# Where split weights lie in SBUF: wider tiles, two starting floats, and two norms side by side

## The chip, the cores and the metric

One core of a Trainium2 chip runs the whole program in one launch. The metric is the device time of one execution in microseconds (us); lower is better.

## The reference, cut to what matters

Two transformer blocks follow each other on 256 tokens of width 1024, all in float32.

```python
def first_block(...):
    ...
    yx, _, _ = mixer_sublayer(hx, kc, vc, rope, ...)
    x = x + g1 * yx
    h2 = modulate(rms_norm(x, norm2_g[l]), sh2, sc2)
    x = x + g2 * expert_choice_moe(h2, w_router[l], w_gate[l], w_up[l], w_down[l])
    return rms_norm(x, final_g)

def second_block(x, p, positions, norm_gains, ...):
    h = x
    for i in range(DEPTH_2):
        g = norm_gains[i]
        f = swiglu(rmsnorm(h, g[0]), ffn_gate[i, 0], ffn_up[i, 0], ffn_down[i, 0])
        h = h + MACARON * rmsnorm(f, g[1])
        mix = hybrid_mixer(rmsnorm(h, g[2]), ...)
        h = h + rmsnorm(mix, g[3])
        f = swiglu(rmsnorm(h, g[4]), ffn_gate[i, 1], ffn_up[i, 1], ffn_down[i, 1])
        h = h + MACARON * rmsnorm(f, g[5])
        gate = jax.nn.sigmoid(rmsnorm(h, g[6]) @ w_ple_gate[i])
        h = h + rmsnorm((p[i].astype(h.dtype) @ w_ple[i]) * gate, g[7])
    return h
```

So the first block's last norm (gain `final_g`) and the second block's first (gain `g[0]`) stand directly behind each other.

## The kernel before

The 256 tokens are two halves `h` of 128. Three stages follow each other: the first block's mixer, its sixteen experts, and the second block, which has two layers of feed-forward, mixer, feed-forward and a gated embedding (`ple`).

Large matrix products are made from split operands. `wsplit` (line 1168) takes a loaded weight tile `wt`, lets ScalarE (ACT) round it to a high part `wh` (line 1180) and VectorE (DVE) subtract that from the tile to give the low part `wl` (line 1181). Activations are split in the same way (`hh`, `hl` and others). `mm3` makes one product from three matmuls:

```python
        mm(out, lw[0], rw[0], start=start, stop=False, skip_group_check=skip)
        mm(out, lw[0], rw[1], start=False, stop=False, skip_group_check=skip)
        mm(out, lw[1], rw[0], start=False, stop=stop, skip_group_check=skip)
```

Its lines are 187, 188 and 189, for all products. The first operand is the stationary one (128 columns of weights for the array), the second moves through it (256 or 512 columns). There are three ways in which split weights are used:
- feature-major: `wh` is stationary, the activations move, 256 columns. This is the middle of each feed-forward (line 1329): column blocks 2 to 10, two halves, gate and up, eight steps `k` each; 864 matmuls in one go per feed-forward. The first mixer's hyena, Fourier and gate columns are made so too.
- token-major by columns (`by_k` and `tok_major`): the activations are stationary, `wh` moves, 256 columns. The first two column blocks of each feed-forward and the mixers' input projections.
- by rows (`rows_linear`): the activations are stationary, `wh` moves, 512 columns. Down, output and gate projections.

The tile pools set where a tile starts. `wh` and `wl` tiles have 1024 floats per partition, so all buffers of one pool start at the same float modulo 256; `shift` puts a small tile ahead of a pool.

At the border between the stages, `moe` adds the experts' sum `acc` to `x1`, half by half, and makes the two norms one behind the other: `norm_rstd` (square with a sum, root, reciprocal), the product with the first gain, then `pre_norm_half` (square, root, reciprocal, product with the gain at line 1212, scaling at 1215, transposes at 1218, split into `hh` and `hl` at 1221 and 1222). Meanwhile the first feed-forward's first four weight blocks (eight tiles) are split, and there `by_k` is given GpSimd (POOL) as the engine for the low parts (line 1309).

The order on each engine comes from the tile framework's scheduler and is fixed when the program is built. SyncE (SP) issues the weight loads in that order into rings of buffers; POOL issues the small loads (gains, embeddings) by the software queue, whose descriptors lie in a scratch area at the start of SBUF.

Of the kernel before, what the change touches and what calls it, by code (L numbers as in the profile page):

```python
# [11 lines left out]
F32 = mybir.dt.float32  # L12
F32R = mybir.dt.float32r
I32 = mybir.dt.int32
AF = mybir.ActivationFunctionType
OP = mybir.AluOpType
# [88 lines left out]
class Builder:  # L105
# [147 lines left out]
    def first_mixer(self, st):  # L253
# [5 lines left out]
        self.shift(WS, 24)  # L259
# [222 lines left out]
        def by_k(w):  # L482

            return [self.wsplit(w[:, 4 * i:4 * i + 4], (4, 256)) for i in range(2)]
# [476 lines left out]
    def moe(self, st):  # L961
# [87 lines left out]
        self.nwide = -1  # L1049
        for h in range(2):  # L1050
            for c in range(2):
                sl = slice(512 * c, 512 * c + 512)
                nc.vector.tensor_tensor(self.x1[:, h, sl], self.x1[:, h, sl], acc[h][c], op=OP.add)
            r = self.norm_rstd(self.h[:, h], self.wide(), D)
            nc.vector.scalar_tensor_tensor(self.h[:, h], self.h[:, h], r, self.fg, op0=OP.mult, op1=OP.mult)
            self.pre_norm_half(h, self.g0)
        self.dbg("h0", self.h)

    def second_tables(self, W):
# [13 lines left out]
        def rest():  # L1073
# [26 lines left out]
            nc.vector.tensor_copy(self.gcol, p[:, :16])  # L1100
            self.eps4 = C.tile([128, 1], F32, name="eps4")
# [3 lines left out]
            for i, t in enumerate((self.fg, self.g0)):  # L1105
                for c in range(2):
                    q = self.trps()
                    nc.tensor.matmul(q, self.ident[:2, i:i + 1].to_broadcast([2, 128]), rows[:, 512 * c:512 * c + 512], start=True, stop=True)
                    nc.vector.tensor_copy(t[:, 512 * c:512 * c + 512], q)

# [55 lines left out]
    def wsplit(self, src, shape, n=D, eng=None):  # L1166

        nc = self.nc
        self.nws += 1
        i = self.nws % sum(c for _, c in self.ws)  # L1170
        for pool, c in self.ws:
            if i < c:
                break
            i -= c
        hi = pool.tile([128, D], F32R, name="wh", tag="wh")[:, :n]
        lo = pool.tile([128, D], F32R, name="wl", tag="wl")[:, :n]
        if shape is not None:
            hi = hi.rearrange("p (a b) -> p a b", a=shape[0])
            lo = lo.rearrange("p (a b) -> p a b", a=shape[0])
        nc.scalar.activation(hi, src, AF.Copy)  # L1180
        (eng or nc.vector).tensor_tensor(lo, src, hi.bitcast(F32), op=OP.subtract)  # L1181
        return hi, lo

    def by_k(self, w, eng=None):

        return [self.wsplit(w[:, 4 * i:4 * i + 4], (4, 256), eng=eng) for i in range(2)]
# [20 lines left out]
    def pre_norm_half(self, h, g):  # L1207
# [4 lines left out]
        nc.vector.tensor_tensor(xn, self.h[:, h], g, op=OP.mult)  # L1212
        for q in range(2):
# [31 lines left out]
    def rows_linear(self, w, nk, lhs, step, tail=None):  # L1245
# [3 lines left out]
        def tile_k(k):  # L1249
            if k % 2 == 0:  # L1250
                ws["raw"] = self.load_rows(w, 128 * k)
            ws[k] = self.wsplit(ws["raw"][:, k % 2], None)
# [27 lines left out]
    def ffn(self, l, i):  # L1280
# [4 lines left out]
        with ExitStack() as FS:  # L1285
            self.shift(FS, 8)
# [19 lines left out]
            for h in range(2):  # L1306
                for c in range(2):
                    if h == 0:
                        pieces.append([self.by_k(self.load_cols(w, 256 * c), nc.gpsimd if l + i == 0 else None)
                                       for w in (wgt, wup)])  # L1310
# [10 lines left out]
            for c in range(2, NF // 2):  # L1321
                wg = self.load_cols(wgt, 256 * c)
                wu = self.load_cols(wup, 256 * c)
                for b in range(2):
                    p = self.gups()
                    for gi, w in ((0, wg), (1, wu)):
                        w2 = self.wsplit(w[:, :, 128 * b:128 * b + 128], (KD, 128))
                        for k in range(KD):
                            self.mm3(p[:, 256 * gi:256 * gi + 256], (w2[0][:, k], w2[1][:, k]), (hh[:, k], hl[:, k]),
                                     k == 0, k == KD - 1, skip=True)  # L1330
# [94 lines left out]
    def mixer(self, l):  # L1425
# [3 lines left out]
        with ExitStack() as XS:  # L1429
            self.shift(XS, 8)  # L1430
# [286 lines left out]
```

## Time and profile before

| | us |
|---|---|
| median of 3 runs | 2335.47 |
| lowest, highest | 2335.37, 2339.55 |
| the profiled execution | 2335.27 |
| its span | 2333.4 |

The profile is of one execution. PE is TensorE's matmuls, PEld its weight loads, which overlap with them. Matmuls are pipelined: one's record lasts longer than the distance to the next one's start. The tables by stretches give busy time, and in brackets the number of instructions that overlap with the stretch; PEclk is the granted clock of TensorE as a share of 2.4 GHz. A line number can be that of a helper.

### The profile page before, as it was taken

To read this page: it belongs to the slowest core of one execution; us is meant where nothing else is said; L and a number is where in the kernel's file an instruction comes from. 1 tells how busy PE (TensorE), PEld (TensorE's weight loads), DVE (VectorE), ACT (ScalarE), POOL (GpSimd) and SP (SyncE) were. 2 spreads that over 40 slices of the span, in tenths; PEclk is the share of its full clock that TensorE was granted. 3 is DMA by queue.
4 is the path that set the end of the run, shared out by engine and by line. 5 is a ranking of instruction groups with operands and counts; after the bars stand their busy time and mean duration, and the time that the engine had idled before them with its cause. 6 is when DMAs were issued, how large, how long until landed. Compare 5 with 4: busy or idle time off the path is not lost.

```text
span 2333.4 us, 31971 instructions
## 1 busy us (share of the span) xinstructions
PE 1913.6 (82%) x13520; PEld 1341.3 (57%) x13520; DVE 922.8 (40%) x1536; ACT 769.1 (33%) x1235; POOL 95.9 (4%) x111
## 2 busy tenths in 40 slices
PE   7899976666656666665656999999999999999998
PEld 4778932111111111111115998879987998879986
DVE  5855630100000000000005555676547654777555
ACT  5544420000000000000004444576437544676444
POOL 2100010000000000000004000100000000100000
PEclk9999988778676867677778999999999999999999
DMA  9466689999999999999997655436555554536551
GB/s 329 158 230 220 254 336 421 425 426 423 425 425 426 424 425 424 425 425 425 424 426 245 210 199 158 140 122 227 182 197 199 181 199 148 181 118 199 181 199 64
DMA packets 201203, 655.76 MB, mean 281 GB/s; under 512 B 10743, under 2 KB 141220, under 8 KB 164196
## 3 DMA queue, kind: packets, MB, share of 16 engines
q1 hardware_dynamic: 196772, 638.99, 71.4%
q0 software_dynamic: 4288, 14.72, 1.9%
q8 instruction: 106, 1.74, 0.3%
q14 instruction: 37, 0.30, 0.0%
HBM read 650.54 MB, written 3.15 MB: 280 GB/s over the span
## 4 chain that ended last, share of the span: by engine, by line
PE 49%; DMA 39%; DVE 6%; ACT 4%; issue 2%; SPq 0%; DVEq 0%; POOL 0%; ACTq 0%; POOLq 0%
DMA wt<-in_w_gate_dram 9%; DMA wp<-in_w_up_dram 9%; PE gu L187 7%; PE gu L188 7%; PE gu L189 7%; DMA wt<-in_w_up_dram 6%; DMA wp<-in_w_down_dram 5%; DMA wt<-in_w_down_dram 5%; DMA wp<-in_w_gate_dram 4%; PE acc L187 4%; PE acc L189 4%; PE acc L188 4%; DVE wl L1181 2%; PE mm L187 2%; PE mm L189 2%
## 5 line engine op out<-in xcount | busy, mean ns | idle before, releaser
L1181 DVE TENSOR_TENSOR wl<-wt,wh 128x1024 fp32r<-128x1024 f32 (+1 forms) x380 | 462.6, 1223 | 279.7 <-ACT wh L1180 277.6
L1180 ACT ACTIVATE wh<-wt 128x1024 fp32r<-128x1024 f32 x388 | 406.2, 1055 | 288.7 <-PE gu L188 112.9
L982 PE MATMUL gu<-wp,xg 128*32 128x512 f32 x1280 | 233.8, 869 | 156.3 <-DMA wp<-in_w_up_dram 99.5
L187 PE MATMUL gu<-hh,wh 128*128 128x256 f32 x1152 | 322.6, 280 | 0.0
L188 PE MATMUL gu<-hl,wh 128*128 128x256 f32 x1152 | 322.2, 280 | 0.0
L189 PE MATMUL gu<-hh,wl 128*128 128x256 f32 x1152 | 321.7, 279 | 0.0
L1007 ACT ACTIVATE a<-gu 128x512 f32<-128x512 f32 x16 | 9.6, 597 | 851.6 <-PE gu L982 851.6
L982 PEld LDWEIGHTS gu<-wp,xg 128*32 128x32 f32 x1280 | 43.4, 137 | 338.1 <-DMA wp<-in_w_up_dram 143.9
L1013 DVE TENSOR_TENSOR a<-a,gu 128x512 f32<-128x512 f32 x16 | 11.0, 688 | 564.4 <-PE gu L982 291.9
L187 PEld LDWEIGHTS gu<-hh,wh 128*128 128x128 f32 x1152 | 216.6, 188 | 0.0
L189 PEld LDWEIGHTS gu<-hh,wl 128*128 128x128 f32 x1152 | 216.2, 188 | 0.0
L188 PEld LDWEIGHTS gu<-hl,wh 128*128 128x128 f32 x1152 | 216.0, 187 | 0.0
L982 PE MATMUL gu<-wt,xg 128*32 128x512 f32 x768 | 129.8, 757 | 68.0 <-DMA wt<-in_w_up_dram 36.1
L1031 PE MATMUL tr<-wp,aT 128*32 128x256 f32 x1280 | 115.7, 525 | 55.4 <-DMA wp<-in_w_down_dram 52.2
L187 PE MATMUL acc<-wh,ah 128*128 128x512 f32 x352 | 139.1, 395 | 0.0
L189 PE MATMUL acc<-wh,al 128*128 128x512 f32 x352 | 138.1, 392 | 0.0
L188 PE MATMUL acc<-wl,ah 128*128 128x512 f32 x352 | 136.7, 388 | 0.0
L1037 DVE TENSOR_TENSOR y<-tr,g2b 32x256 f32<-32x256 f32 x64 | 26.9, 420 | 260.2 <-PE tr L1031 259.5
L1031 PEld LDWEIGHTS tr<-wp,aT 128*32 128x32 f32 x1280 | 50.1, 144 | 120.3 <-DMA wp<-in_w_down_dram 69.0
L982 PEld LDWEIGHTS gu<-wt,xg 128*32 128x32 f32 x768 | 20.3, 124 | 167.6 <-DMA wt<-in_w_gate_dram 76.2
L187 PE MATMUL acc<-wh,hh 128*128 128x256 f32 (+1 forms) x304 | 102.0, 336 | 1.1 <-ACT vd L1455 1.1
L189 PE MATMUL acc<-wh,hl 128*128 128x256 f32 (+1 forms) x304 | 99.2, 326 | 0.5 <-DVE hl L1222 0.5
(464 smaller groups left out, 3158.5 us busy)
## 6 DMA issues: line engine op xcount, KB each, us to landing
wp<-in_w_up_dram SPq DMA_DIRECT2D x48, 2048.0 KB, 27.5
wp<-in_w_down_dram SPq DMA_DIRECT2D x40, 2048.0 KB, 27.1
wt<-in_w_gate_dram SPq DMA_DIRECT2D x64, 1024.0 KB, 27.3
wp<-in_w_gate_dram SPq DMA_DIRECT2D x32, 2048.0 KB, 27.6
wt<-in_w_down_dram SPq DMA_DIRECT2D x48, 1024.0 KB, 27.6
wt<-in_ffn_gate_dram SPq DMA_DIRECT2D x44, 1024.0 KB, 6.5
wt<-in_ffn_up_dram SPq DMA_DIRECT2D x44, 1024.0 KB, 5.3
wt<-in_ffn_down_dram SPq DMA_DIRECT2D x44, 1024.0 KB, 4.9
```

The lines of the kernel that those rows point to most:

```text
L187: mm(out, lw[0], rw[0], start=start, stop=False, skip_group_check=skip)
L188: mm(out, lw[0], rw[1], start=False, stop=False, skip_group_check=skip)
L189: mm(out, lw[1], rw[0], start=False, stop=stop, skip_group_check=skip)
L982: mm((pga, pup)[g][32 * j:32 * j + 32, :], xg[2 * a + i][:, 32 * e:32 * e + 32], w[:, 512 * j:512 * j + 512], start=(done[g] == 1), stop=( ...
L1007: silu = nc.scalar.activation(a, pga, AF.Silu)
L1013: mul = nc.vector.tensor_tensor(a, a, pup, op=OP.mult)
L1031: mm(pd[32 * c:32 * c + 32, :256], aT[:, 2 * i + b, 32 * j:32 * j + 32], w[:, 1024 * b + 256 * c:1024 * b + 256 * c + 256], start=(t == 0) ...
L1037: nc.vector.tensor_tensor(y4[32 * r:32 * r + 32, 256 * c:256 * c + 256], pd[32 * c:32 * c + 32, :256], self.g2b[32 * c:32 * c + 32, 256 * ...
L1180: nc.scalar.activation(hi, src, AF.Copy)
L1181: (eng or nc.vector).tensor_tensor(lo, src, hi.bitcast(F32), op=OP.subtract)
```

## The change

Tiles of split weights are 64 floats wider (1088), so that successive buffers start 64 floats apart modulo 256, and `wsplit` places its 1024 floats at float 0 or 32 of the tile, by the argument `off`. The `shift` tiles change. The software queue's scratch is 4096 bytes per partition in place of 16384, which makes room. At the border, squares of the sum and of its product with the first gain are made side by side by halves of 512 columns; the second norm's root comes from both sums, its operand from the product of both gains (`fgg`, made in the expert stage), and the first norm's result `h` is written afterwards. The eight low parts that POOL made go to DVE. Scaling, transposes and split are now a function of their own, `to_operand`, with the same instructions.

```diff
@@ first_mixer
-        self.shift(WS, 24)
+        self.shift(WS, 56)
...
-            return [self.wsplit(w[:, 4 * i:4 * i + 4], (4, 256)) for i in range(2)]
+            return [self.wsplit(w[:, 4 * i:4 * i + 4], (4, 256), off=32) for i in range(2)]
@@ moe
         for h in range(2):
+            hv, xn = self.wide(), self.wide()
+            ms = W.tile([128, 2, 2], F32, name="ms", bufs=2)
             for c in range(2):
                 sl = slice(512 * c, 512 * c + 512)
-                nc.vector.tensor_tensor(self.x1[:, h, sl], self.x1[:, h, sl], acc[h][c], op=OP.add)
-            r = self.norm_rstd(self.h[:, h], self.wide(), D)
-            nc.vector.scalar_tensor_tensor(self.h[:, h], self.h[:, h], r, self.fg, op0=OP.mult, op1=OP.mult)
-            self.pre_norm_half(h, self.g0)
+                x2 = self.x1[:, h, sl]
+                nc.vector.tensor_tensor(x2, x2, acc[h][c], op=OP.add)
+                junk = W.tile([128, 512], F32, name="a")
+                nc.scalar.activation(junk, x2, AF.Square, scale=D ** -0.5, accum_out=ms[:, 0, c:c + 1])
+                nc.vector.tensor_tensor(hv[:, sl], x2, self.fg[:, sl], op=OP.mult)
+                nc.scalar.activation(hv[:, sl], hv[:, sl], AF.Square, scale=D ** -0.5, accum_out=ms[:, 1, c:c + 1])
+                nc.vector.tensor_tensor(xn[:, sl], x2, self.fgg[:, sl], op=OP.mult)
+            m = W.tile([128, 4], F32, name="mm", bufs=2)
+            nc.vector.tensor_tensor(m[:, 0:2], ms[:, :, 0], ms[:, :, 1], op=OP.add)
+            nc.vector.scalar_tensor_tensor(m[:, 2:3], m[:, 0:1], EPS, m[:, 1:2], op0=OP.mult, op1=OP.add)
+            nc.scalar.activation(m[:, 2:3], m[:, 2:3], AF.Sqrt, bias=self.eps2, scale=1.0)
+            nc.vector.reciprocal(m[:, 2:3], m[:, 2:3])
+            self.to_operand(h, xn, m[:, 2:3])
+            nc.scalar.activation(m[:, 3:4], m[:, 0:1], AF.Sqrt, bias=self.eps, scale=1.0)
+            nc.vector.reciprocal(m[:, 3:4], m[:, 3:4])
+            nc.vector.scalar_tensor_tensor(self.h[:, h], self.h[:, h], m[:, 3:4], self.fg, op0=OP.mult, op1=OP.mult)
@@ second_tables
+            self.fgg = W.tile([128, D], F32, name="fgg", bufs=1)
+            nc.vector.tensor_tensor(self.fgg, self.fg, self.g0, op=OP.mult)
@@ wsplit
-        hi = pool.tile([128, D], F32R, name="wh", tag="wh")[:, :n]
-        lo = pool.tile([128, D], F32R, name="wl", tag="wl")[:, :n]
+        hi = pool.tile([128, D + 64], F32R, name="wh", tag="wh")[:, off:off + n]
+        lo = pool.tile([128, D + 64], F32R, name="wl", tag="wl")[:, off:off + n]
...
-        (eng or nc.vector).tensor_tensor(lo, src, hi.bitcast(F32), op=OP.subtract)
+        nc.vector.tensor_tensor(lo, src, hi.bitcast(F32), op=OP.subtract)
@@ pre_norm_half
         nc.vector.tensor_tensor(xn, self.h[:, h], g, op=OP.mult)
+        self.to_operand(h, xn, r)
+
+    def to_operand(self, h, xn, r):
...
@@ rows_linear
-            ws[k] = self.wsplit(ws["raw"][:, k % 2], None)
+            ws[k] = self.wsplit(ws["raw"][:, k % 2], None, off=32)
@@ ffn
-            self.shift(FS, 8)
+            self.shift(FS, 48)
...
-                        pieces.append([self.by_k(self.load_cols(w, 256 * c), nc.gpsimd if l + i == 0 else None)
-                                       for w in (wgt, wup)])
+                        pieces.append([self.by_k(self.load_cols(w, 256 * c)) for w in (wgt, wup)])
...
-                        w2 = self.wsplit(w[:, :, 128 * b:128 * b + 128], (KD, 128))
+                        w2 = self.wsplit(w[:, :, 128 * b:128 * b + 128], (KD, 128), off=32)
@@ mixer
-            self.shift(XS, 8)
+            self.shift(XS, 16)
@@ kernel
-    nc = _bacc.Bacc("TRN2", target_bir_lowering=False, num_devices=1)
+    nc = _bacc.Bacc("TRN2", target_bir_lowering=False, num_devices=1, dynamic_dma_scratch_size=4096)
```

Distances as the pools place the tiles: start of the moving operand less start of the stationary operand of the next matmul, in floats of a partition, modulo 128 (from one `k` to the next it moves by 128). In brackets, matmuls in the whole program that are followed by another of their kind.

| moving, then stationary | columns | before | now |
|---|---|---|---|
| `hh`, `hl` on `wh`, `wl`: feed-forward's middle (3448) | 256 | 16 | 48, 112 |
| `wh`, `wl` on `hh`, `hl`: token-major, second block (1444) | 256 | 112 | 48, 112 |
| `wh`, `wl` on `ah`, `al`: down projection (1048) | 512 | 80 | 0, 64 |
| `wh`, `wl` on `hh`, `hl`: output and gate projection (382) | 512 | 112 | 16, 80 |
| `xh`, `xl` on `wh`, `wl`: first mixer, early (327) | 256 | 16 | 48, 112 |
| the same, later (431) | 256 | 48 | 48, 112 |
| `wh`, `wl` on `xh`, `xl`: first mixer, q, k, v (139) | 256 | 112 | 48, 112 |
| `wh`, `wl` on `mT`: first output projection (91) | 512 | 0, 80 | 0, 16, 64, 80 |

The order of instructions differs at the border alone. DVE before, from the add of the experts' sum to the second half's scaling (`x_70` is `x1`, `nr` a reciprocal root, `nt` a work tile):

```order
L1053 TENSOR_TENSOR x_70<-x_70,acc 128x512 x4
L1204 RECIPROCAL nr<-nr 128x1
L1055 SCALAR_TENSOR_TENSOR x_70<-x_70,nr,gain 128x1024
L1212 TENSOR_TENSOR nt<-x_70,gain 128x1024
L1204 RECIPROCAL nr<-nr 128x1
L1215 TENSOR_SCALAR nt<-nt,nr 128x512 x2
L1222 TENSOR_TENSOR hl<-tr,hh 128x4x128
L1204 RECIPROCAL nr<-nr 128x1
L1055 SCALAR_TENSOR_TENSOR x_70<-x_70,nr,gain 128x1024
L1222 TENSOR_TENSOR hl<-tr,hh 128x4x128
L1212 TENSOR_TENSOR nt<-x_70,gain 128x1024
```

DVE now, the same place, from the second half's first sums to the second column block's first low parts:

```order
L1240 TENSOR_SCALAR nt<-nt,mm 128x512 x2
L1072 SCALAR_TENSOR_TENSOR x_70<-x_70,mm,gain 128x1024
L1065 TENSOR_TENSOR mm<-ms 128x2
L1201 TENSOR_TENSOR wl<-wt,wh 128x1024
L1247 TENSOR_TENSOR hl<-tr,hh 128x4x128 x2
L1063 TENSOR_TENSOR nt<-x_70,fgg 128x512 x2
L1066 SCALAR_TENSOR_TENSOR mm<-mm 128x1
L1071 RECIPROCAL mm<-mm 128x1
L1201 TENSOR_TENSOR wl<-wt,wh 128x1024
L1068 RECIPROCAL mm<-mm 128x1
L1072 SCALAR_TENSOR_TENSOR x_70<-x_70,mm,gain 128x1024
L1240 TENSOR_SCALAR nt<-nt,mm 128x512 x2
```

The products at 1063 and the low parts at 1201 have come in between; the product with the first gain (1055, now 1072) stands behind the scaling.

POOL before, at the same place:

```order
L1071 DMA grows<-in_norm_gains_dram 1x16x64
L1181 TENSOR_TENSOR wl<-wt,wh 128x1024 x7
L1115 DMA gain<-in_norm_gains_dram 128x1024
L1181 TENSOR_TENSOR wl<-wt,wh 128x1024
L1115 DMA gain<-in_norm_gains_dram 128x1024
```

POOL now:

```order
L1087 DMA grows<-in_norm_gains_dram 1x16x64
L1135 DMA gain<-in_norm_gains_dram 128x1024 x2
L1500 DMA lg<-in_q_norm_dram 128x256
L1501 DMA lg<-in_kv_norm_dram 128x128
L1586 MEMSET qz 128x2048
```

The eight low parts are gone from POOL, and the two gain loads stand first.

## Rows read from the trace of the kernel before

**Rows 1.** The page: busy time with its share, and PE's busy tenths by slice.

```profile
PE 1913.6 (82%) x13520; PEld 1341.3 (57%) x13520; DVE 922.8 (40%) x1536; ACT 769.1 (33%) x1235; POOL 95.9 (4%) x111
...
PE   7899976666656666665656999999999999999998
```

**Rows 2.** The chain that ended last, at the border: start us, us, what.

```profile
1242.01 1.30 DVE x L1053 x2
...
1251.10 4.88 DVE nt L1215 x2
...
1265.26 1.10 PE tr L1218 x8
```

**Rows 3.** PE by stretches: us, busy (x), PEclk, DMA share, GB/s; feed-forward's middles.

```profile
1290.00:1380.00 90.00, 90.00 (x766) 1.00 0.58 194
...
2142.00:2232.00 90.00, 90.00 (x767) 1.00 0.58 196
```

**Rows 4.** Instructions in order of time, in a middle: start us, us, engine, line.

```profile
1380.02 0.28 PE L187 MATMUL gu<-hh,wh 128*128 128x256 f32 x1
1380.02 0.19 PEld L188 LDWEIGHTS gu<-hl,wh 128*128 128x128 f32 x1
```

**Rows 5.** PE by stretches, other 256-column runs; distances: 112, 16, 48, 48, 112, 112.

```profile
48.00:60.80 12.80, 12.80 (x116) 1.00 1.09 355
91.00:104.00 13.00, 13.00 (x113) 1.00 0.73 259
193.00:208.00 15.00, 15.00 (x130) 1.00 0.92 276
215.00:267.00 52.00, 52.00 (x461) 1.00 0.61 196
...
1459.20:1467.00 7.80, 7.80 (x68) 1.00 0.60 202
...
2134.30:2139.20 4.90, 4.90 (x46) 1.00 0.94 298
```

**Rows 6.** PE in order of time, entry into the last feed-forward's middle.

```profile
2138.48 0.28 PE L187 MATMUL gu<-hh,wh 128*128 128x256 f32 x1
...
2139.16 0.28 PE L187 MATMUL gu<-hh,wh 128*128 128x256 f32 x1
...
2140.09 0.28 PE L188 MATMUL gu<-hl,wh 128*128 128x256 f32 x1
...
2140.80 0.28 PE L188 MATMUL gu<-hl,wh 128*128 128x256 f32 x1
```

**Rows 7.** PE with 512 columns, in order of time, then a down projection by stretches.

```profile
277.39 0.39 PE L187 MATMUL wo<-wh,mT 128*128 128x512 f32 x1
...
280.57 0.39 PE L189 MATMUL wo<-wh,mT 128*128 128x512 f32 x1
...
1558.95 0.39 PE L187 MATMUL acc<-wh,hh 128*128 128x512 f32 x1
...
1575.75 0.39 PE L187 MATMUL acc<-wh,hh 128*128 128x512 f32 x1
...
1388.00:1445.00 57.00, 57.00 (x250) 1.00 0.46 149
```

**Rows 8.** Groups by line at the border (1238 to 1268 us): busy us, mean ns.

```profile
L1181 POOL TENSOR_TENSOR wl<-wt,wh 128x1024 fp32r<-128x1024 f32 x8 | 22.4, 2821 | 895.5 <-ACT wh L1180 895.4
...
L1215 DVE TENSOR_SCALAR nt<-nt,nr 128x512 f32<-128x512 f32 x4 | 7.7, 1968 | 0.1
```

**Rows 9.** Groups by line and form, border and second block (from 1230 us).

```profile
L1181 DVE TENSOR_TENSOR wl<-wt,wh 128x1024 fp32r<-128x1024 f32 x322 | 393.3, 1226 | 240.1 <-ACT wh L1180 238.0
...
L1222 DVE TENSOR_TENSOR hl<-tr,hh 128x512 fp32r<-128x512 f32 x32 | 20.7, 685 | 7.0 <-ACT hh L1221 7.0
L1215 DVE TENSOR_SCALAR nt<-nt,nr 128x512 f32<-128x512 f32 x32 | 20.1, 670 | 0.2
...
L1204 DVE RECIPROCAL nr<-nr 128x1 f32<-128x1 f32 x33 | 5.2, 157 | 5.6 <-ACT nr L1203 4.0 <-ACT nr L1201 1.5
```

More of the change, by code (lines that the diff above doesn't have):

```diff
@@ L1100, in rest @@
             nc.vector.tensor_copy(self.gcol, p[:, :16])
+            self.eps2 = C.tile([128, 1], F32, name="eps2")
+            nc.vector.memset(self.eps2, EPS * EPS)
             self.eps4 = C.tile([128, 1], F32, name="eps4")
@@ L1164, in wide, with wsplit @@
         return pool.tile([128, D], F32, name="nt", tag=tag, bufs=3 if tag == "nt" else 1)
-    def wsplit(self, src, shape, n=D, eng=None):
+    def wsplit(self, src, shape, n=D, off=0):
         nc = self.nc
@@ L1180, in wsplit, with by_k @@
         nc.scalar.activation(hi, src, AF.Copy)
-        (eng or nc.vector).tensor_tensor(lo, src, hi.bitcast(F32), op=OP.subtract)
+        nc.vector.tensor_tensor(lo, src, hi.bitcast(F32), op=OP.subtract)
         return hi, lo
-    def by_k(self, w, eng=None):
-        return [self.wsplit(w[:, 4 * i:4 * i + 4], (4, 256), eng=eng) for i in range(2)]
+    def by_k(self, w):
+        return [self.wsplit(w[:, 4 * i:4 * i + 4], (4, 256)) for i in range(2)]
     def tok_major(self, out, h, pieces):
@@ L1212, in pre_norm_half @@
         nc.vector.tensor_tensor(xn, self.h[:, h], g, op=OP.mult)
+        self.to_operand(h, xn, r)
+    def to_operand(self, h, xn, r):
+        nc = self.nc
         for q in range(2):
```

## The prediction

> **What bounds the kernel now.** I read the page's busy shares and slices first. TensorE (PE) is busy in 82% of the span: at nine tenths in slices 3 to 5, the first mixer, at five or six from slice 7 to 22, and at nine from slice 23 on, the second block [rows 1]. In the middle the expert stage waits for weights, and no edit moves those. So the change is worth what it does to PE in the first mixer and in the second block, and at the border between the two, where PE idles.
>
> That border I read in the chain of waits [rows 2]. From 1242.01 us, when the experts' sum is complete, to 1265.26, when the second half's transposes start, the chain is on VectorE (DVE): adds, the two norms, scalings. The reader is to see 4.88 us for two scalings of 128x512.
>
> In the second block I asked how fast PE goes while it waits for nothing. The table by stretches counts the matmuls of each stretch; since a matmul lasts 0.28 us (0.39 with 512 columns) and one that began just before is counted too, the pitch from one start to the next is (stretch + duration) / count. In the feed-forward's middle, four stretches of 90 us: 90.28 / 766 or 767 = **117.8 ns** for 256 columns, at clock 1.00, PE never idle [rows 3]. 256 columns at 2.4 GHz are 106.7 ns. So some 11 ns per matmul are neither columns nor waiting.
>
> What else goes on in a matmul's time is the next one's weight load: both records start at the same moment [rows 4]. Both read SBUF, the moving operand along one row of floats and the weights along another, so the distance of these two, which the change sets, is a possible cause. I therefore read the pitch of the same instruction elsewhere against the distances in the table of the change. At 16 (modulo 128) 13.28 / 113 = 117.5. At 48 it is 52.28 / 461 = 113.4 over 52 us, but also 15.28 / 130 = 117.5 over 15 us. At 112 it is 13.08 / 116 = 112.8, 8.08 / 68 = 118.8, 5.18 / 46 = 112.6 [rows 5]. Of 17 such stretches at 48 or 112 ten lie near 113 and seven near 118; the row shows its first, its last and the clearest. So there are **two speeds**, and a stretch keeps the one it has. Entering the last feed-forward the pitch is 113 (six matmuls in 0.68 us) although the distance is already 16; after one pause for a transpose it is 118 (six in 0.71), and stays so [rows 6]. All four middles begin with such a pause and all four are slow. So at 16 a pause ends at 118 ns each time I can see, at 48 or 112 in less than half of them.
>
> With 512 columns there is no such memory, and the distance shows plainly. At 0: 14 matmuls from 277.39 to 280.57, 227.1 ns. At 112: 72 from 1558.95 to 1575.75, 233.3 ns. At 80, the down projection: 57.39 / 250 = 229.6, and 228.6 with the 251 that one of the four gives; I take 229 [rows 7].
>
> **The parts.** One profiled execution took 2335.27 us; the sum is made against that. It is 0.2 us under the median of the runs, which is 2335.47.
>
> 1. Feed-forward middles. 3448 matmuls go from 16 to 48 and 112. Bounds: nothing (the pitch stays at 117.8) and 3448 x (117.8 - 113.4) = 15.2 us. I take 15.2: the long stretch at 48 is the nearest row, it too goes through hundreds of matmuls. DVE and ScalarE have time for it; a tile of 24 matmuls would take 2.72 us, and its split 1.23 us on DVE [rows 9]; DMA moves 194 to 196 GB/s there [rows 3].
>
> The rule that speaks against this part: the Trainium skill, page "SBUF — State Buffer", section "SBUF: two separate sides", has contention on the engine side only at the port pair that VectorE and GpSimd share, and says that TensorE never waits on anyone; a later section gives it a second, independent read port for weight loads. By that, the distance would be worth nothing and parts 1 to 3 would be 0. The trace speaks against it where distance alone differs, 227.1, 229 and 233.3 ns [rows 7].
>
> 2. Rows. The down projections' 1048 matmuls go from 80 to 0 and 64: 1048 x (229 - 227.1) = 2.0 us. Output and gate projections, 382 at 112, go to 16 and 80: 382 x (233.3 - 229) = 1.6 us. No row has 16 or 64 with 512 columns; bounds are 227.1 and 233.3, so from 4.4 us gained to 4.5 lost on the first (half of them at 64) and the second together; I take each as its neighbour modulo 64, as 48 and 112 behave alike.
>
> 3. First mixer: 327 matmuls with xh and xl go from 16 to 48 and 112, at most 327 x 4.4 = 1.4 us. PE is the chain there; I take 1.
>
> 4. Token-major columns, 1444 matmuls, stay at 48 or 112: 0, with 1444 x 4.4 / 2 = 3 us either way, as runs fall on the one or the other pitch.
>
> 5. Border. GpSimd's eight lo splits, 2821 ns each, go to DVE at 1226 [rows 8, 9], 9.8 us more for DVE. While GpSimd ran them, DVE's four scalings took 1968 ns each [rows 8]; all 32 of the block have 20.1 us, so the other 28 have (20.1 - 7.7) / 28 = 0.44 [rows 9]. New DVE work up to the eighth split: four adds, eight products, four hi/lo differences of 128x512 at 0.685 (11.0 us), four scalings at 0.44 (1.8), two 128x1024 products at a split's 1.23 (2.5), nine small ones at a reciprocal's 0.157 (1.4), eight splits (9.8) and two 128x256 items of the first column block (0.7, at half a 128x512 each) [rows 9]: 27.2 us, so from 1242.0 to 1269.2. PE then lacks 12 matmuls of the second column block: 1270.6. Before, that block began at 1266.11, after eight transposes [rows 2], and took 48 x 0.1156 = 5.5 us, the mean of the two speeds: 1271.6. So **1 us** gained; the first matmuls come sooner, but behind them stands the queue of splits. Bounds: 4 us gained, if PE's order hides the late splits, and 3 lost, if each small step between ScalarE and DVE stalls DVE's queue, which is served in order. The norms' own order (the second root no longer behind the first) is inside this.
>
> 6. The product of the two gains (1.2 us, as a split) and a memset lie in the expert stage, where DVE idles. The smaller DMA scratch and the wider tiles give no engine work; if the software queue's ring became too short, GpSimd's issues would wait. The same DMAs are issued in the same order on SP. I take 0.
>
> Sum: 15.2 + 2.0 + 1.6 + 1.0 + 1.0 = 20.8 us; 2335.3 - 20.8 = **2314.5 us**.
>
> **Rivals.**
> B. The middles are fast in part: two of the four, or half of each, 7.6 us less gain: 2322. For it: one pause decides, and at 112 both outcomes occur [rows 5].
> C. The state, not the distance, rules 256 columns, and the pauses that open the middles leave them slow as before. Part 1 is 0: 2335.3 - 5.6 = 2329.7. If distance is worth nothing anywhere, only the border is left: 2334.3. (That is the time by the Trainium skill's rule of part 1, which the 512-column rows contradict.) For C: all four middles agree now, at the same place of the program, as if the kind of pause decided; and 16 gave 113 for some matmuls [rows 6]. Against: 16 with a pause is never seen fast.
> D. Slower. Before, each stream had one distance; now each tile of 1088 floats moves it by 64. If every such step is a new chance for 118 ns, streams that are fast now become slow: of the 1444 token-major matmuls the fast half, 3.2 us; the first mixer's 461 of the long stretch at 48 [rows 5], 2.0 us; the down projection's half at 64 as bad as 112, 524 x 4.3 = 2.3 us; the middles gain nothing and the border gives 1. Together 2335.3 + 6.5 = 2342. It decides when a stream cannot keep 113 ns over one tile, that is 24 matmuls. Against: in the fast stretches both distances modulo 256 follow each other all the time, and 512 columns change speed within three matmuls.
>
> **How the numbers follow.** Forecast 0.52, B 0.20, C 0.19, D 0.09. A measurement of this kernel tells some 0.2%, 4.7 us, from no change. The forecast's own range, with parts 2, 4 and 5 at their bounds, is 2308 to 2320. To hold 8 in 10 the range must take in B and the part of C that keeps parts 2 and 3: 2308 to 2332. Faster by over 0.2% (under 2330.8) are the forecast, B and half of C: 0.81; within 0.2% the rest of C and a sliver of D: 0.11; slower 0.08.
>
> **What would show it.** Right: the four middles at 90.28 / 113.4 = 796 matmuls in 90 us in place of 766; the down projection's 57 us stretch with 252 or 253; output projection at 229; no GpSimd split, DVE's scalings at 0.44 at the border, and the first middle's start 1 us sooner. Wrong: a count of 766 in the middles (C), a mixture among the four (B), token-major stretches all at 118 or down at 233 (D), or PE waiting at the border for a lo tile beyond 1271 us.

## The result and the profile after

| | before | after |
|---|---|---|
| median, us | 2335.98 | 2312.84 |
| the profiled execution | 2335.27 | 2310.14 |
| its span | 2333.4 | 2308.4 |

The ratio is 0.9894 with a 95% interval of 0.9875 to 0.9913: faster by 1.1%. One of the four executions after was slow (2828.68 us, granted clock 0.63); it is in the median of the table but not in the ratio, which goes by the other three, with a median of 2311.20 us. Forecast were 2314.5 us and 20.8 us of gain; the profiled executions differ by 25.1.

The page after, busy time and PE's busy tenths by slice:

```profile
PE 1875.6 (81%) x13520; PEld 1322.4 (57%) x13520; DVE 923.0 (40%) x1556; ACT 768.1 (33%) x1243; POOL 73.7 (3%) x103
...
PE   7899966656556655665556999899999999999998
```

PE does the same 13520 matmuls in 38 us less busy time (1913.6 in [rows 1]); DVE's busy time is the same although it has eight low parts more. Not all of the 38 us is gain: 14.0 of it are the experts' matmuls at L982 (363.6 us before, 349.6 after), in a stage that waits for weights. What is gain shows in the stretches after, the four middles and one down projection (us, then busy time with the number of instructions for PE, PEld, DVE, ACT and POOL, then PEclk, DMA share, GB/s):

```profile
1284.00:1374.00 90.00, 90.00 (x796) 90.00 (x795) 52.76 (x67) 44.56 (x66) 0.00 (x0) 1.00 0.60 202
1596.00:1686.00 90.00, 90.00 (x796) 90.00 (x796) 52.76 (x66) 44.53 (x66) 0.00 (x0) 1.00 0.61 202
1810.00:1900.00 90.00, 90.00 (x796) 90.00 (x796) 52.77 (x66) 44.61 (x66) 0.00 (x0) 1.00 0.62 205
2122.00:2212.00 90.00, 90.00 (x796) 90.00 (x796) 52.67 (x66) 44.51 (x67) 0.00 (x0) 1.00 0.62 206
...
1378.00:1435.00 57.00, 57.00 (x253) 47.21 (x252) 26.44 (x26) 24.36 (x30) 0.00 (x0) 1.00 0.45 145
```

766 or 767 matmuls in 90 us [rows 3] have become 796, the number forecast: 90.28 / 796 = 113.4 ns, at the same clock. The down projection has 253 in 57 us where [rows 7] has 250: 57.39 / 253 = 226.8 ns.

The border, PE in order of time, from the experts' last gather products (L1042) over the second norm's transposes to the first token-major matmul, and the first matmul of the first middle:

```profile
1238.89 3.74 PE L1042 MATMUL acc<-y,back 128*128 128x512 f32 x8 [0.97 <-DVE y L1037]
1248.23 1.94 PE L1243 MATMUL tr<-ident,nt 128*128 128x128 f32 x8 [5.59 <-DVE nt L1240]
1250.75 0.58 PE L187 MATMUL gu<-wh,hh 128*128 128x256 f32 x1 [0.58 <-ACT hh L1246]
...
1278.62 0.28 PE L187 MATMUL gu<-hh,wh 128*128 128x256 f32 x1
```

I call the distance from the first L1042 to the first middle "the border": 1278.62 - 1238.89 = 39.7 us. In the trace before it runs from 1239.95 to 1285.61, 45.7. The border is 5.9 us shorter, and 5.0 of that lie ahead of the first token-major matmul (11.86 us behind L1042, before 1256.80 - 1239.95 = 16.85). These are one execution each; a second one of the change has 40.9 us (below), so a difference of about a microsecond between borders tells nothing.

### The profile page after: what moved, and what is told of

The parts are those of the page before. It is cut to its first block, busy times and chain, and to the rows that moved or that the text cites. A ratio compares the mean times of both kernels' runs of the same rounds, so it can differ in the third digit from the quotient of the medians.

```text
span 2308.4 us, 31994 instructions
## 1 busy us (share of the span) xinstructions
PE 1875.6 (81%) x13520; PEld 1322.4 (57%) x13520; DVE 923.0 (40%) x1556; ACT 768.1 (33%) x1243; POOL 73.7 (3%) x103
## 4 chain that ended last, share of the span: by engine, by line
PE 49%; DMA 40%; DVE 6%; ACT 4%; issue 1%; SPq 0%; DVEq 0%; POOL 0%; ACTq 0%; POOLq 0%
DMA wt<-in_w_gate_dram 10%; DMA wp<-in_w_up_dram 7%; PE gu L187 7%; PE gu L189 7%; PE gu L188 7%; DMA wt<-in_w_down_dram 6%; DMA wp<-in_w_down_dram 6%; DMA wt<-in_w_up_dram 5%; PE acc L187 4%; PE acc L189 4%; PE acc L188 4%; DMA wp<-in_w_gate_dram 2%; DVE wl L1201 2%; PE mm L187 1%; PE mm L189 1%
## 5 line engine op out<-in xcount | busy, mean ns | idle before, releaser
L1201 DVE TENSOR_TENSOR wl<-wt,wh 128x1024 fp32r<-128x1024 f32 x388 | 472.1, 1223 | 264.8 <-ACT wh L1200 261.6
L982 PE MATMUL gu<-wp,xg 128*32 128x512 f32 x1280 | 227.2, 847 | 157.8 <-DMA wp<-in_w_up_dram 103.2
L982 PEld LDWEIGHTS gu<-wp,xg 128*32 128x32 f32 x1280 | 42.8, 135 | 335.7 <-DMA wp<-in_w_up_dram 144.4
L982 PE MATMUL gu<-wt,xg 128*32 128x512 f32 x768 | 122.4, 716 | 78.2 <-DMA wt<-in_w_up_dram 41.3
L982 PEld LDWEIGHTS gu<-wt,xg 128*32 128x32 f32 x768 | 19.5, 121 | 170.6 <-DMA wt<-in_w_gate_dram 79.3
L187 PE MATMUL gu<-wh,hh 128*128 128x256 f32 (+1 forms) x336 | 98.4, 294 | 1.1 <-ACT hh L1246 1.1
```

Of the source, the lines that this page charges most:

```text
L982: mm((pga, pup)[g][32 * j:32 * j + 32, :], xg[2 * a + i][:, 32 * e:32 * e + 32], w[:, 512 * j:512 * j + 512], start=(done[g] == 1), stop=( ...
L1201: nc.vector.tensor_tensor(lo, src, hi.bitcast(F32), op=OP.subtract)
```

## The experiments

Two questions were open. Is it the distance of the operands that sets the pitch, and not the pause ahead of a stretch (rival C) or the stepping of the buffers (rival D)? And what made the border gain 5.9 us where 1.0 was forecast?

### Maps of the distance

`e1_map_a` and `e2_map_b` make the tiles of the second block 1152 floats wide, a multiple of 128, so that no buffer steps, and choose the starting float by a table, for each feed-forward or mixer and each use:

```diff
-                        w2 = self.wsplit(w[:, :, 128 * b:128 * b + 128], (KD, 128), off=32)
+                        w2 = self.wsplit(w[:, :, 128 * b:128 * b + 128], (KD, 128), off=OFF['mid'][2 * l + i])
-        hi = pool.tile([128, D + 64], F32R, name="wh", tag="wh")[:, off:off + n]
+        hi = pool.tile([128, wd], F32R, name="wh", tag="wh")[:, off:off + n]
```

The low part's tile, token-major columns and rows are edited alike.

> The changed kernel, with split tiles of the second block 128 floats wider (so every buffer has the same start modulo 128) and the starting float chosen per use: the four feed-forward middles get the distances 0, 32, 64, 96, the four down projections 32, 96, 48, 16, the output and gate projections 0, 64, 32, 96. Theory A, the distance of the moving operand to the next stationary one sets the pitch: the four middles differ from each other although the same instructions run in the same places; a distance keeps one pitch through 800 matmuls, 113.4 or 117.8 ns or a third value; with 512 columns 227 to 233.4 ns, each projection at one value. Theory C, the pause that opens a middle decides and not the distance: all four middles agree, at 117.8 as before the change or at 113.4 as after it, and 512 columns too show nothing that goes with the distance. Theory D, it is the stepping of buffers by 64 floats that keeps the middles fast: without stepping all four are at 117.8.

> As the run before, with middles at 80, 48, 16, 112, down projections at 112, 64, 0, 80, output and gate projections at 48, 112, 16, 80. Theory A: the third middle (16) at 117.8 ns, the second (48) and the fourth (112) at 113.4, the first (80) not known; the down projections at 233.4, 227, 227.1 and 229 ns in this order. Theory C: all four middles alike, whichever. Theory D: all four at 117.8, since no buffer steps. A middle at 16 that runs at 113.4, or one at 48 at 117.8, refutes A.

The stretches of the first map, middles at 0, 32, 64, 96:

```profile
1290.00:1380.00 90.00, 90.00 (x752) 90.00 (x751) 49.91 (x63) 42.46 (x64) 0.00 (x0) 1.00 0.57 187
1608.00:1698.00 90.00, 90.00 (x761) 90.00 (x760) 50.70 (x63) 42.10 (x63) 0.00 (x0) 1.00 0.59 196
1830.00:1920.00 90.00, 90.00 (x752) 90.00 (x751) 50.07 (x63) 41.87 (x62) 0.00 (x0) 1.00 0.58 191
2152.00:2242.00 90.00, 90.00 (x761) 90.00 (x760) 50.27 (x64) 42.94 (x64) 0.00 (x0) 1.00 0.58 190
```

Of the second map, middles at 80, 48, 16, 112, then down projections at 112, 64, 0, 80:

```profile
1286.00:1376.00 90.00, 90.00 (x767) 90.00 (x766) 51.12 (x64) 42.90 (x64) 0.00 (x0) 1.00 0.58 193
1606.00:1696.00 90.00, 90.00 (x796) 90.00 (x796) 52.78 (x66) 44.54 (x66) 0.00 (x0) 1.00 0.61 205
1820.00:1910.00 90.00, 90.00 (x766) 90.00 (x765) 50.92 (x63) 42.68 (x64) 0.00 (x0) 1.00 0.59 196
2136.00:2226.00 90.00, 90.00 (x796) 90.00 (x795) 52.78 (x66) 44.27 (x65) 0.00 (x0) 1.00 0.62 204
...
1384.50:1441.50 57.00, 57.00 (x246) 45.94 (x245) 24.99 (x23) 22.95 (x28) 0.00 (x0) 1.00 0.45 144
1700.80:1757.80 57.00, 57.00 (x253) 47.21 (x252) 26.43 (x26) 24.36 (x30) 0.00 (x0) 1.00 0.45 149
1919.30:1976.30 57.00, 57.00 (x253) 47.20 (x252) 26.43 (x26) 24.34 (x30) 0.00 (x0) 1.00 0.45 144
2232.40:2289.40 57.00, 57.00 (x251) 46.77 (x250) 25.88 (x25) 23.88 (x29) 0.00 (x0) 1.00 0.39 131
```

The same instructions, in the same places of one program, at clock 1.00 with PE never idle: 752, 761, 767 or 796 in 90 us, by the distance alone. In ns, with a period of 64 floats, since 64 gives what 0 gives and so on:

| distance modulo 64 | 0 | 16 | 32 | 48 |
|---|---|---|---|---|
| 256 columns | 120.0 | 117.8 | 118.7 | 113.4 |
| 512 columns | 226.8 | 229 | 232.3 | 233.3 |

(512 columns at 32 and 48 from the first map's down projections: 247 and 246 in 57 us.) Each map was run once; the times were 2344.27 and 2325.94 us. For the middles and for 512 columns theory A stands, C and D fall: the second middle of `e2_map_b` is at 113.4 with buffers that don't step, its third at 117.8.

In the middles only the weights moved, since `hh` and `hl` start at the same float modulo 64 in all runs. So it could be the weights' own place that counts, and not the distance. The token-major columns of the two maps speak against that: there the weights are the moving operand, and start elsewhere for the same distance. At 0, in the mixer of the second block's first layer of `e2_map_b`, the stretch is

```profile
1459.00:1464.00 5.00, 5.00 (x44) 5.00 (x43) 1.92 (x2) 3.35 (x7) 0.00 (x0) 1.00 0.28 96
```

5.28 / 44 = 120.0 ns; at 16 most stretches of the maps are at 117.8, at 32 they are at 118.5 to 119.0, about as in the middles. The order is opposite for the two widths: 48 is best for 256 columns and worst for 512. So weights that serve both need two places, which is what the argument `off` gives.

`e5_map_c` and `e6_map_d` are the same kernel with other numbers in the table.

> The kernel of the first two maps with finer steps: the four middles at 40, 44, 52, 56, the down projections at 4, 8, 56, 60, token-major columns of the feed-forwards at the middles' distances, of the mixers at 36 and 60, output projections at 8 and 56, gate projections at 4 and 60. The two maps gave, at 0, 16, 32, 48 modulo 64, for 256 columns 120.0, 117.8, 118.7 and 113.4 ns, for 512 columns 227, 229, 232.3 and 233.3. If the pitch is a smooth function of the distance with a period of 64 floats, 40 and 44 lie between 118.7 and 113.4, 52 and 56 between 113.4 and 120.0, and 4, 8, 56, 60 with 512 columns between 227 and 229 or 227 and 233.3. If only the class of 16 floats counts (a block that operands share), 40, 44 equal 32 or 48, and 52, 56, 60 equal 48: steps, not slopes. A distance where 256 columns are faster than 113.4, or one without the second pitch of 117.8, would be worth moving to.

> As the run before, with middles at 60, 36, 24, 8, down projections at 40, 24, 12, 20, token-major columns of the feed-forwards at 60, 36, 46, 50, of the mixers at 54 and 42, output projections at 2 and 62, gate projections at 6 and 40. Smooth: 60 near 118 to 120, 36 near 118, 24 between 117.8 and 118.7, 8 between 117.8 and 120. Steps of 16: 60 at 113.4 like 48, 36 at 118.7 like 32, 24 at 117.8 like 16, 8 at 120.0 like 0.

Between the multiples of 16 nothing is smooth, and nothing better (2341.93 and 2341.75 us). Middles in 85 us, `e5_map_c` at 52, the worst that was seen:

```profile
1830.00:1915.00 85.00, 85.00 (x691) 85.00 (x690) 46.02 (x60) 39.20 (x58) 0.00 (x0) 1.00 0.55 179
```

and `e6_map_d` at 60 and at 8:

```profile
1290.00:1375.00 85.00, 85.00 (x720) 85.00 (x720) 47.95 (x60) 40.27 (x61) 0.00 (x0) 1.00 0.58 194
...
2153.00:2238.00 85.00, 85.00 (x731) 85.00 (x730) 48.95 (x62) 40.58 (x61) 0.00 (x0) 1.00 0.58 192
```

85.28 / 691 = 123.4, 85.28 / 720 = 118.4, 85.28 / 731 = 116.7 ns. The others lie at 118.4 to 119.9, and both forecasts missed: with a slope 52 would lie below 120.0 and 8 above 117.8, with steps of 16 the distances 52, 56 and 60 would give 113.4. With 512 columns a down projection at 60 runs at 226.8 like one at 0, but a gate projection at 60 (35 matmuls of `e5_map_c`, from 2309.44 to 2317.48 us) at 236.5, which the expectation of `e12_map_e` puts at 234.5. Both have the same distance and other starts. So off the multiples of 16 the distance does not tell the pitch.

`e12_map_e` asks the same on the multiples: the down projection's operands and weights both move by 8 floats, middles stay at 48.

```diff
-            self.shift(FS, 48)
+            self.shift(FS, 56)
```

> The kernel of the maps with the down projection's operands moved by 8 floats, and the weights with them: the four down projections have the distances 0, 16, 32, 48 as in the maps, but both operands start at multiples of 16 floats, where all starts so far were at 8 more. Middles all at 48, token-major columns at 48 and 112, output and gate projections at 0 and 64. If the distance alone counts: 227, 229, 232.3 and 233.3 ns. If the start itself counts (which would explain why distances between the multiples of 16 gave 226.8 at 60 in one place and 234.5 in another), at least one of the four is elsewhere by over 1 ns. For what decides between 113.4 and 117.8 at 48: if a fixed place of every buffer were enough, all token-major stretches agree; if the pause decides anew each time, they are mixed as in the change, and the middles are at 113.4 four times of four again.

Its down projections, at 0, 16, 32, 48:

```profile
1381.80:1438.80 57.00, 57.00 (x253) 47.23 (x252) 26.41 (x26) 24.35 (x30) 0.00 (x0) 1.00 0.45 146
1693.90:1750.90 57.00, 57.00 (x251) 46.77 (x250) 25.88 (x25) 23.88 (x29) 0.00 (x0) 1.00 0.44 150
1907.40:1964.40 57.00, 57.00 (x247) 46.23 (x246) 25.17 (x24) 23.15 (x28) 0.00 (x0) 1.00 0.45 145
2221.00:2278.00 57.00, 57.00 (x246) 45.94 (x245) 24.94 (x23) 22.96 (x28) 0.00 (x0) 1.00 0.38 131
```

253, 251, 247, 246: the same four values (2315.36 us in all, one run). With 512 columns and distances that are multiples of 16 the distance is enough in all down projections, wherever the pair lies. Among the output and gate projections of the maps one doesn't fit by 1 ns: the last gate projection of `e1_map_a`, at 96, has 233.4 where 32 and 96 have 232.3 to 232.4 elsewhere; why stays open.

### Two numbers alone

`e9_two_numbers` is the kernel before, tiles 1024 wide, with

```diff
-        self.shift(st, 16, "right")
+        self.shift(st, 48, "right")
...
-            self.shift(FS, 8)
+            self.shift(FS, 56)
```

> The kernel before with two numbers changed: the small tile ahead of the second block's split tiles has 48 floats in place of 16, the one ahead of the down projection's operands 56 in place of 8. Tiles stay 1024 floats wide, no starting float, scratch and border as before. Distances: middles 48, down projections 0, output and gate projections 80, token-major columns 80 (before 112). Theory A by the maps: middles 3448 x 4.4 = 15.2 us, down 1048 x 2.2 = 2.3, output and gate 382 x 4.2 = 1.6 gained, token-major 1444 at 116 to 117.8 in place of 115.2, 1 to 3.8 us lost: 2318 to 2321 against 2335.3, ratio 0.993 to 0.994. If wide tiles and the starting float are what the gain needs, nothing or little is gained.

Measured were 2321.94 us beside 2338.13 for the kernel before, ratio 0.9931 (0.9917 to 0.9946), which is within theory A's 0.993 to 0.994. Its first middle:

```profile
1292.00:1382.00 90.00, 90.00 (x796) 90.00 (x795) 52.55 (x65) 44.53 (x66) 0.00 (x0) 1.00 0.62 206
```

The middles gain all they can. The price is in the token-major matmuls, which now have 80: those that follow each other directly average 117.7 ns, 115.2 before the change, and 1444 x 2.5 is 3.6 us lost. By the ratios, wide tiles and the starting float are worth what lies between 0.9931 here and 0.9912 for the whole layout without the new border (next section), some 4 us: they buy these back, no more. Since the scratch is that of before, a smaller one isn't what the middles gain by.

### The border

`e3_border_only` puts the new border, with the small scratch, into the kernel before; two shift tiles keep its distances. `e4_layout_only` puts the border of before into the changed kernel, whose small scratch it keeps.

```diff
@@ e3_border_only, against before
+            (the changed kernel's lines in moe, eps2, fgg, to_operand)
-                        pieces.append([self.by_k(self.load_cols(w, 256 * c), nc.gpsimd if l + i == 0 else None)
+                        pieces.append([self.by_k(self.load_cols(w, 256 * c), None)
-            self.shift(FS, 8)
+            self.shift(FS, 128)
-            self.shift(XS, 8)
+            self.shift(XS, 128)
@@ e4_layout_only, against the change: the reverse, in moe and in by_k
```

> The kernel before with the border alone changed: norms side by side, the eight low parts on VectorE, the small scratch; tiles, starting floats and distances as before. By the prediction's sum the border is worth 1.0 us: 2334.3. By the trace of the change, in which the first middle's start gained 5.8 us more than the experts' end did, it is worth 5.8 us: 2329.5, ratio 0.9975. In both the four middles stay at 117.8 ns and the down projections at 229. If the border's gain came from the distances (first column blocks faster), it would be absent here: 2335.

> The changed kernel with the border of before put back: norms one behind the other, the eight low parts on GpSimd; distances as in the change. Theory A: middles at 113.4 ns, down projections at 227; 15.2 + 2.0 + 1.6 + 1.0 = 19.8 us gained, 2315.5, ratio 0.9915. If a part of the gain in the middles needs the other border (order of buffers, state handed on), the first middle is at 117.8 and the time 3.8 us more, 2319.3. If parts add up, this run's gain and that of the border alone sum to the change's 23 to 25 us.

The border alone: 2332.19 us, ratio 0.9977 (0.9968 to 0.9987), some 5.4 us gained, not 1.0. The layout alone: 2317.42 us, ratio 0.9912 (0.9897 to 0.9926), 20.6 us gained, where theory A said 19.8. Together 26.0, and the change gives 24.8 (0.0106 x 2336): the parts add up within the intervals.

`e7_pool_lo` and `e8_old_norm` are the change with one half of the border put back: the low parts on GpSimd, or the norms one behind the other.

```diff
@@ e7_pool_lo
-                        pieces.append([self.by_k(self.load_cols(w, 256 * c)) for w in (wgt, wup)])
+                        pieces.append([self.by_k(self.load_cols(w, 256 * c), nc.gpsimd if l + i == 0 else None)
+                                       for w in (wgt, wup)])
@@ e8_old_norm: the lines of before in moe
```

> The changed kernel with the eight low parts back on GpSimd, the norms still side by side. From the experts' last gather product to the first middle the kernel before takes 45.8 us, the changed one 39.9, the border alone changed 39.8, the layout alone changed 46.7. Theory P, the gain is VectorE's, which GpSimd slowed (scalings at 1.97 us against 0.44): with the low parts back on GpSimd this is 44 to 47 us, and VectorE's 128x512 products and scalings show more than 1 us again. Theory N, the gain is the second root that no longer waits for the first: it stays within 1 us of 40.

> The changed kernel with the two norms one behind the other as before, the eight low parts on VectorE. Theory P: VectorE runs at its own pace, the border takes 40 to 42 us. Theory N: 44 to 46 us. If both edits are needed, this run and the one with the low parts on GpSimd both lie at 43 or above; if either is enough, both lie near 40.

The expectations counted to the second matmul of the middle; here to the first, 0.1 us less. The border in us, one profiled execution each (the maps have the new border too, with other distances of the token-major columns, and take 39.9 to 41.8):

| | low parts on GpSimd | low parts on VectorE |
|---|---|---|
| norms one behind the other | 45.7 (before), 46.6 (`e4_layout_only`), 47.4 (`e9_two_numbers`) | 43.9 (`e8_old_norm`) |
| norms side by side | 51.6 (`e7_pool_lo`) | 39.7 (after), 39.6 (`e3_border_only`), 40.9 (`e11_change_again`, below) |

The times were 2325.09 us for `e7_pool_lo` and 2317.51 for `e8_old_norm`, one run each. Neither theory has both numbers; that both edits are needed was expected to show as two borders of 43 or above, and does. Side by side alone costs some 5 or 6 us (51.6 against 46.6 or 45.7). Moving the low parts alone saves 2 or 3, little more than executions of one kernel differ by. Both together save 5 to 7. The small scratch alone gains nothing here: `e4_layout_only` has it too. The groups of `e7_pool_lo` at the border (1236 to 1285 us; busy us, mean ns) say why:

```profile
L1201 POOL TENSOR_TENSOR wl<-wt,wh 128x1024 fp32r<-128x1024 f32 x8 | 20.7, 2605 | 794.4 <-DMA wt<-in_ffn_up_dram 788.5 <-ACT wh L1200 6.0
...
L1061 DVE TENSOR_TENSOR nt<-x,gain 128x512 f32<-128x512 f32 x4 | 7.9, 1986 | 0.0
L1240 DVE TENSOR_SCALAR nt<-nt,mm 128x512 f32<-128x512 f32 x4 | 5.8, 1478 | 0.0
...
L1247 DVE TENSOR_TENSOR hl<-tr,hh 128x512 fp32r<-128x512 f32 x4 | 2.6, 680 | 0.1
L1058 DVE TENSOR_TENSOR x<-x,acc 128x512 f32<-128x512 f32 x4 | 2.6, 680 | 1.2 <-PE acc L1042 1.2
```

and in the change, at the same place:

```profile
L1061 DVE TENSOR_TENSOR nt<-x,gain 128x512 f32<-128x512 f32 x4 | 2.7, 681 | 0.0
...
L1058 DVE TENSOR_TENSOR x<-x,acc 128x512 f32<-128x512 f32 x4 | 2.6, 682 | 0.0
...
L1247 DVE TENSOR_TENSOR hl<-tr,hh 128x512 fp32r<-128x512 f32 x4 | 2.6, 684 | 0.7 <-ACT hh L1246 0.7
L1240 DVE TENSOR_SCALAR nt<-nt,mm 128x512 f32<-128x512 f32 x4 | 1.8, 479 | 0.0
```

While GpSimd makes low parts, a product of two SBUF tiles takes DVE 1986 ns on the mean in place of 681, a scaling 1478 in place of 479; an operation of the same shape with one operand in PSUM (`acc`, `tr`) takes its 680 in either. The Trainium skill, page "SBUF — State Buffer", section "SBUF: two separate sides", has VectorE's operations with two SBUF inputs or in a two-port mode and GpSimd's exclude each other at a shared port, for a whole instruction; these rows agree. The new norms make four products of 512 columns per half ahead of the transposes, all of the kind that is held up. So the new norms need the low parts gone from GpSimd, and moving the low parts is worth most with the new norms.

### A version beside the change

`e10_best` brings output and gate projections to 0 and 64 by `off=16`, and writes the first norm's two results behind the first four column blocks. `e11_change_again` is the changed kernel itself.

```diff
-            nc.vector.scalar_tensor_tensor(self.h[:, h], self.h[:, h], m[:, 3:4], self.fg, op0=OP.mult, op1=OP.mult)
+            self.late.append((h, m))
...
             self.mark("ffnm")
+            for h, m in self.late:
+                nc.vector.scalar_tensor_tensor(self.h[:, h], self.h[:, h], m[:, 3:4], self.fg, op0=OP.mult, op1=OP.mult)
+            self.late = []
```

> The changed kernel with output and gate projections at 0 and 64 in place of 16 and 80 (382 x 2.1 = 0.8 us), and the first norm's two results, 1.27 us each on VectorE, written after the first four column blocks instead of between the norms. If the border is VectorE's to the eighth low part, as the prediction had it, the first middle starts 2.5 us sooner, 37.4 us behind the experts' last gather product in place of 39.9; if TensorE's own matmuls set it, nothing. Together 0.8 to 3.3 us less than the changed kernel in the same call.

> The changed kernel itself, beside the run before on the same chip: 0.9894 of the kernel before, within its interval, 0.9875 to 0.9913.

Measured: 2310.18 us, ratio 0.9884 (0.9869 to 0.9899), beside 2312.95 us and 0.9892 (0.9876 to 0.9909) for the change. The intervals overlap, so that it beats the change is not shown. The trace shows the first part: output and gate projections are at 227.7 ns in place of 229.1. The border is 38.9 us in this execution, 39.7 and 40.9 in two of the change, so how much DVE's 2.5 us were worth is not resolved; the 37.4 that were expected are not reached. What the trace does show is that PE waits for no low part any more, 1.4 us once in the change: from there on its own matmuls set the border.

## Why the prediction was right, point by point

**1. Middles.** 15.2 us forecast from 3448 x 4.4. The distances from matmul to matmul over the four middles sum to 406.3 us before and 391.4 after: 14.9. The rule weighed against this part would have given 0, and middles that differ by the distance alone, 752 to 796 in 90 us, contradict it. Rival B rested on "at 112 both outcomes occur"; but every middle at 48 or 112, in all the runs, is at 113.4: 34 of 34. The share of outcomes in shorter stretches did not carry over to the middles; what spares them is not known.

**2. Rows.** Down 2.0 forecast, 240.3 - 238.0 = 2.3 measured; output and gate 1.6 forecast, 91.9 - 90.3 = 1.6 measured. Taking 64 as 0 and 16 as 80 was a guess from 48 and 112; the maps show the period of 64, so this was a lucky guess.

**3 and 6.** 1 us forecast up to the end of the experts; the first L1042 starts at 1238.89 in place of 1239.95, 1.1 us sooner. The first mixer's output projection starts 2.7 us sooner, at 267 us, and 1.6 of that are gone at the end of the expert stage, which waits for weights. But this is within what executions differ by: in the eleven that have the new first mixer L1042 starts between 1238.60 and 1242.43, in the three that have the old one between 1239.95 and 1242.98. The forecast is neither borne out nor refuted.

**4. Token-major.** 0 forecast, 3 us either way. With everything else subtracted, 25.1 - 14.9 - 2.3 - 1.6 - 1.1 - 5.9 = -0.7 is left for it and the end, one execution against one. Since a stretch can change its pitch from one execution to the next (last section), a sum near 0 is chance.

**5. Border.** This term was mis-sized: 1.0 forecast with 4 as its upper bound, 5.9 measured. Both ends of its sum were wrong, by two and by three times the term. The first is "27.2 us, so from 1242.0 to 1269.2". DVE after, at the border, in order of time, first low part and adds, two products, and the last low part:

```profile
1240.01 1.23 DVE L1201 TENSOR_TENSOR wl<-wt,wh 128x1024 fp32r<-128x1024 f32 x1 [0.27 <-ACT wh L1200]
1241.27 1.28 DVE L1058 TENSOR_TENSOR x<-x,acc 128x512 f32<-128x512 f32 x2
1242.47 0.69 DVE L1061 TENSOR_TENSOR nt<-x,gain 128x512 f32<-128x512 f32 x1
1243.07 0.68 DVE L1063 TENSOR_TENSOR nt<-x,fgg 128x512 f32<-128x512 f32 x1
...
1263.73 1.22 DVE L1201 TENSOR_TENSOR wl<-wt,wh 128x1024 fp32r<-128x1024 f32 x1
```

The eighth low part ends at 1264.95, 23.7 us behind the first add. One low part (1.2 us) ran ahead of the adds. The rest is overlap: the products' records last 0.68 us but start 0.60 apart, and the sum took durations for DVE where for PE it had taken the pitch.

The second is the end of the second column block before: "1266.11, after eight transposes" and "48 x 0.1156 = 5.5 us" gave 1271.6. Before, token-major matmuls from the last transposes to the end of that block (us, busy, PEclk, DMA share, GB/s):

```profile
1266.11:1273.67 7.56, 7.56 (x63) 1.00 0.62 208
```

They are 63, not 48: in the program's order 19 of the first column block and 44 of the second stand behind these transposes. The block ends at 1273.67. After, it ends at 1266.73. Counted from the first add, the end of the second block is 31.7 us away before (29.6 by the forecast) and 25.5 after (28.6); these 2.1 and 3.1 us are what the term lacks.

Then "behind them stands the queue of splits" failed too: PE waited for a low part once. PE's waits after, from 1238 to 1280 us:

```profile
PE tr L1243 <- DVE nt L1240: 5.6, 1, 5.6
PE gu L188 <- DVE wl L1201: 1.4, 1, 1.4
```

Before, it waited 14.1 us for the scalings. When PE came to the twelve matmuls of the eighth low part, at 1265.32, that had been ready for 0.4 us. What covers the low parts is PE's own work, which begins 5.0 us sooner, and part of it at half speed. Stretches after, PEclk:

```profile
1251.00:1253.00 2.00, 2.00 (x10) 1.94 (x11) 2.00 (x4) 2.00 (x4) 0.00 (x0) 0.50 0.46 69
...
1255.00:1258.00 3.00, 3.00 (x30) 3.00 (x28) 2.73 (x4) 0.23 (x1) 0.62 (x1) 1.00 0.32 116
```

Behind an idle time of 5.59 us the granted clock is 0.50, 1.2 GHz, and a matmul takes 0.21 us; from 1255 on it is 1.00.

In sum the mechanisms of parts 1 and 2 were right and their sizes good to 0.3 us. At the border the gain came from where it was looked for, scalings that GpSimd no longer holds up and a start of PE that comes sooner; that DVE's queue would take this back was wrong.

One reading of the range is wrong as well: "with parts 2, 4 and 5 at their bounds" does not end at 2320. With 4.5 us lost in part 2 in place of 3.6 gained, 3 lost in part 4 and 3 lost in place of 1 gained in part 5 it ends at 2329.6. Nothing hung on it, since the result lies below the forecast.

## What to carry to other kernels

Where TensorE is never idle and the pitch of its matmuls still is some 10% above columns over clock (117.8 against 106.7 ns here), read the pitch by (stretch + duration) / count and compare stretches by where their two operands start: here 16 floats more or less were worth up to 6%. For float32 tiles in multiples of 16 floats, distance modulo 64, 48 was best with 256 columns and 0 with 512; weights that serve both ways need a place for each. When work moves off GpSimd, or a norm is cut into more VectorE products, look at which of VectorE's operations read two SBUF tiles while GpSimd runs: one edit that costs time alone (some 5 us here) and one that saves little can be worth more together than either. And add durations only where records don't overlap.

## What was not expected of the hardware

At 48 or 112 a stretch of 256 columns, the middles apart, has either 113.4 or 117.8 ns, mostly from its first matmuls on, and what decides it stays open. It is not the program: in the first mixer, the same 69 token-major matmuls at the same addresses have 117.8 ns in one execution of the change (from 45.46 to 53.47 us),

```profile
46.00:53.00 7.00, 7.00 (x61) 7.00 (x61) 4.02 (x7) 5.36 (x10) 2.01 (x3) 1.00 1.09 360
```

and 113.5 in `e11_change_again`, the same kernel (from 47.53 to 55.25 us, in this stretch with what follows them),

```profile
48.00:60.00 12.00, 12.00 (x108) 12.00 (x107) 9.64 (x14) 8.77 (x16) 3.62 (x4) 1.00 1.10 353
```

12.28 / 108 = 113.7. It is not the token-major form either: the first mixer's run of 121 feature-major matmuls at 48 and 112 is at 113.4 in the change (88.49 to 102.10 us) and at 117.8 in `e10_best` (89.97 to 104.10). Nor is it 48 alone: at 80, which goes with 16, the mixer of the second block's second layer in `e1_map_a` has 43 matmuls at 113.3 (1992.40 to 1997.16 us) and, right behind a pause for transposes, 23 (2044.44 to 2046.93 us), so that the prediction's "16 with a pause is never seen fast" does not hold for short stretches. Of the second block's 38 token-major stretches (12 or more matmuls, each within 0.16 us of the last) 14 run at 117 to 118 in the change and 12 in `e12_map_e`, where buffers don't step: stepping is not the cause. Some 3 us of the kernel hang on it, by the estimate of part 4. Why the distance matters at all, and why the order turns round between 256 and 512 columns, no run here shows. Nor was it tried whether a clock kept up through the border would gain anything.
